# Two more weight places in a pool of their own, so that three output-projection tiles are split ahead of the layer norm's operands

## The chip, the cores and the metric

The kernel runs on one core of one Trainium2 chip. The metric is device time in microseconds (us) from one launch to its end. Three runs of the kernel before gave 1234.79, 1235.42 and 1237.09 us, a median of 1235.42 us. The profile is one further execution, with its own time.

## The reference

The reference is one step of a two-layer encoder over 576 rows: 512 frames of a new stream and 64 frames of a running one. Layer 0 mixes time with a causal depthwise convolution, layer 1 with stick-breaking attention, and each is followed by a SwiGLU feed-forward. The change touches the convolution module, which in the reference is:

```python
def conv_module(xn, prefix, w_in, b_in, w_dw, b_dw, ln_g, ln_b, w_out, b_out):
    a, gate = jnp.split(xn @ w_in + b_in, 2, axis=-1)
    u = a * jax.nn.sigmoid(gate)
    u_ext = jnp.concatenate([prefix.astype(u.dtype), u], axis=1)
    y = lax.conv_general_dilated(u_ext, w_dw[:, None, :], window_strides=(1,), padding='VALID', ...) + b_dw
    y = jax.nn.silu(layernorm(y, ln_g, ln_b))
    return y @ w_out + b_out, u_ext[:, -CONV_STATE:]
```

`D_MODEL` is 1024, the convolution has 31 taps, and all inputs are float32. The output projection `y @ w_out` needs every one of the 1024 layer-normed channels for each of its outputs, and no channel is layer-normed before the sums over all 1024 are known.

## The kernel before

**Layout.** Everything lies transposed: channels on the 128 partitions, the 576 rows of time along the free axis. 1024 channels are 8 chunks `c` (or `m`, for outputs). A product's 576 columns are taken as two halves of 288.

**Split operands.** A float32 product is made of three fp32r products. Each operand x is a rounded high part and the rest, x = xh + xl, and the matmuls are wh·xh, wh·xl and wl·xh. So one weight chunk against one operand chunk is 3 × 2 = 6 matmuls of 128x288 (`mm_ops`, line 591). The weights are split on the chip as they come: a raw tile of 128x1024 lands by DMA in one of the places `wr0` to `wr2` (`load_raw`, line 313). From there it is split in two *units* of 128x512: ScalarE (ACT) writes the high part `wh` (line 509), and VectorE (DVE) subtracts it from the raw weights into `wl` (line 519). With a free PSUM bank a first ACT copy goes to the bank `hp` (line 514), and DVE reads that. A unit sits in a place `w0` to `w3` (tiles `wh0`/`wl0` and so on) until the last matmul that reads it has run.

**Places.** `free["w"]` lists the free places. `advance` takes a place for the next unit as soon as the matmuls of an earlier tile are in the program; `place_for` gives out only places named in `WPOOL` for units *ahead*, those that belong to the next section of the program, because `WPOOL` tiles live in a pool `wpool` that outlasts a section. Section 0 is the projection `w_in`, the convolution and the layer norm. Section 1 is the output projection `w_out` and feed-forward 0, in which `ffn` adds two places, `w4` and `w5`, from its own pool `act0`, which takes over the memory of the convolution's pool. One tile is two units, so 4 places hold two tiles of `w_out`.

**Order.** The instructions are recorded as operations with costs, and `Plan` lays each engine's order out ahead, section by section, from these costs. Engines run their own queues in that order and wait by semaphores. The cost `"next"` (line 1266) stands in the plan of section 0 for the work that TensorE (PE) will find behind each layer-normed chunk.

**Section 0.** For each chunk, `project` makes the gate and value products `pg` and `pa`, `gate` and `glu` make `u`, and the 31 taps are either done on DVE (`acc`, line 1045) and, in part, on ACT and GpSimd (`pr`, `pacc`, lines 1059 and 1062), or on PE (`py`, chunks 4, 5, 7). Then PE sums over channels into `cl` (line 978). ACT and DVE make the mean (`nmp`) and the inverse root (`rp`) of 152 sums from it, and PE spreads both over time (`nm`, `rt`, line 1185). Between these PE runs products of ones, `warm` (line 774), that nobody reads. Then each chunk c is normed: DVE adds the mean (line 1228) and multiplies by the root (line 1236) into `zf`, ACT takes the silu (line 1240) and the high part `zh` (line 1246), and DVE, or GpSimd for chunks 2, 4 and 6, takes the low part `zl` (line 1250). Chunk 0 goes in two halves.

**Section 1.** `w_out_tile` makes the output tiles `po_m` in the order 0, 4, 1, 5, 2, 6, 3, 7, each from all 8 chunks `zh`/`zl`, and adds them to `h` (line 741). The gate and up products `pg` (line 591, then `j_A`, `j_B`, `j_C`, line 1404) follow.

Of the kernel before, what the change touches and what calls it, by code (L numbers as in the profile page):

```python
# [10 lines left out]
P = 128  # L11
# [80 lines left out]

ALONE = (1, 7, 6, 4, 5, 2, 3)
WPOOL = {f"{q}{i}" for q in ("w", "wh", "wl") for i in range(4)} | {f"wr{i}" for i in range(3)}
N_S = 4

FIRST = ((("b0", "b1"), ("b4", "b5")), (("b4", "b5"), ("b0", "b1")))
# [121 lines left out]
def build(tc, xT, vec, st, stp, bdp, wt, ck, cv, w_in, w_out, gu, down, wk, wv, wq, wo, yT, csp, css, kp, ks, vp, vs):  # L219
# [5 lines left out]
    wpool = ctx.enter_context(tc.tile_pool(name="wpool", bufs=1))  # L225
    xpool = ctx.enter_context(tc.tile_pool(name="xpool", bufs=1))
    kpool = ctx.enter_context(tc.tile_pool(name="kpool", bufs=1))
    dram = ctx.enter_context(tc.tile_pool(name="dram", bufs=1, space=bass.MemoryType.DRAM))
    psum = []

# [83 lines left out]

    def wide(tag):

        return wpool if tag in WPOOL else cur[0]

    vecs = base.tile([P, NV], F32, name="vecs")
    nc.sync.dma_start(vecs[:, :V_DW], vec[:, :V_DW])  # L320
# [39 lines left out]
    def dve(n, ptr=False):  # L360
        return n / 960 + (0.13 if ptr else 0.07)
# [4 lines left out]
    def pe(n):  # L366
        return n * 0.000442 + 0.004
# [17 lines left out]


    lo_eng = ["DVE"]
    free = {"wr": [], "w": ["w0", "w1", "w2", "w3"], "S": []}
    pos = {"src": 3, "unit": 0, "tile": 0, "end": 0}
    raw_at = {i: f"wr{i}" for i in range(3)}  # L390
    unit_at, last_use = {}, {}
# [6 lines left out]
    def place_for(q, ahead):  # L398

        for t in free[q]:  # L400
            if not ahead or t in WPOOL:
                free[q].remove(t)
                return t

# [143 lines left out]
    def section():  # L548

        pos["end"] += 1  # L550
        hbanks.clear()
        for q in free:
            free[q] = [t for t in free[q] if t in WPOOL]

    def by_part(tag):
        return [(tag, 0), (tag, 1)]
# [407 lines left out]
        phase_sums(c)  # L964

    stats, psums = [], []

    def stat(parts, dep, i, bias=0.0):

# [15 lines left out]
    def phase_sums(c):  # L985

        k = POLY.index(c)
        et, sqt = f"ye{k % 2}", "zq1" if psums else "zq0"
        es = [et] + [(et, b) for b in range(2)]
        if c == LAST:  # L990
            for b in range(2):

                def f(b=b):
                    if not b:
                        tile(("sq", c), "zq1", (P, Q, QW))
                    nc.scalar.activation(X[("sq", c)][:, 2 * b : 2 * b + 2, :], X[("ye", c)][:, 2 * b : 2 * b + 2, :], AF.Square)

                def pair(key, b=b):
                    x = X[(key, c)]
                    o = tile((key + "2", c, b), f"{key}2{b}", (P, QW))  # L1000
                    nc.vector.tensor_tensor(o, x[:, 2 * b, :], x[:, 2 * b + 1, :], op=ALU.add)

                op("ACT", act(2 * QW, False), f, reads=[(et, b), et] + ["zq1"] * b, writes=[("zq1", b)] + ["zq1"] * (not b), urgent=True)
                for i, (key, deps) in enumerate((("ye", [et, (et, b)]), ("sq", ["zq1", ("zq1", b)]))):
                    op("DVE", dve(QW), lambda key=key, pair=pair: pair(key), reads=deps, writes=[f"{key}2{b}"], urgent=True, port=True)
                    stat([((lambda: sum_of), (lambda key=key, b=b: X[(key + "2", c, b)]))], [f"{key}2{b}"], i)
            return
        op("ACT", act(YW, False), lambda: nc.scalar.activation(tile(("sq", c), sqt, (P, Q, QW)), X[("ye", c)], AF.Square), reads=es, writes=[sqt])
        psums.append(c)
        a = psums[0]  # L1010
        if len(psums) == 2:
            ea = f"ye{POLY.index(a) % 2}"
            op("Pool", pool(YW), lambda: nc.gpsimd.tensor_tensor(tile(("yes",), "yes", (P, Q, QW)), X[("ye", a)], X[("ye", c)], op=ALU.add),
               reads=es + [ea] + [(ea, b) for b in range(2)], writes=["yes"])
        elif len(psums) > 2:
            op("Pool", pool(YW), lambda: nc.gpsimd.tensor_tensor(X[("yes",)], X[("yes",)], X[("ye", c)], op=ALU.add), reads=es, writes=["yes"])
        if len(psums) > 1:
            op("Pool", pool(YW), lambda: nc.gpsimd.tensor_tensor(X[("sq", a)], X[("sq", a)], X[("sq", c)], op=ALU.add), reads=[sqt], writes=["zq0"])
        if len(psums) == len(POLY) - (LAST in POLY):
            for i, (key, tag) in enumerate(((("yes",), "yes"), (("sq", a), "zq0"))):  # L1020
                for n in (2, 1):

                    def f(key=key, n=n):
                        x = X[key]
                        nc.gpsimd.tensor_tensor(x[:, 0:n, :], x[:, 0:n, :], x[:, n : 2 * n, :], op=ALU.add)

                    op("Pool", pool(n * QW), f, writes=[tag])
                stat([((lambda: sum_of), (lambda key=key: X[key][:, 0, :]))], [tag], i)
# [234 lines left out]


    for c in range(NC):
        op("next", 6 * pe(HA) * 2, None, reads=[("z", c, "h"), ("z", c, "l"), ("z", c, "h", 1), ("z", c, "l", 1)], writes=["next"])
    flush()
    section()
    conv_pool.close()
# [169 lines left out]
    def ffn(l, mixer, g_next, nrm_next, x_busy, k_busy):  # L1439
# [1 line left out]
        ap = pool_.enter_context(tc.tile_pool(name=f"act{l}", bufs=1, reuse_waits="tile"))  # L1441
        cur[0] = ap
        free["wr"].append("wr3")
        free["w"] += [f"w{i}" for i in range(4, N_W)]
        free["S"] += [f"S{i}" for i in range(N_S)]
        spots["f"] = [f"f{i}" for i in range(N_F)]
        spots["x"] = [t for t in XT if t not in x_busy]
# [351 lines left out]

    nkv = Norm("kv")  # L1800
    ffn(0, w_out_tile, V_KVG, nkv, XT, [])


    att_pool = ExitStack()
# [641 lines left out]
```

## Time and profile before

| | us |
|---|---|
| runs of the kernel before | 1234.79, 1235.42, 1237.09 (median 1235.42) |
| the profiled execution | 1235.88, of which the span from first to last instruction is 1234.1 |
| PE busy over the span | 1208.9 |
| DVE, ACT, GpSimd busy | 981.4, 979.9, 769.0 |
| granted TensorE clock, mean | 0.994 |

The profile names an engine, a line of the kernel, an operation and tiles (out<-in). In a timeline row the first number is the start and the second how long the row's instructions took, from the first one's start to the last one's end; `x` counts them. A bracket gives the idle time of the engine just before the row and what ended it. Rows of one engine overlap by up to some tenths, since an instruction is recorded to its end while the next has begun; the distance between two starts is what counts in a sum. PE is also pipelined: a product of 288 columns shows 0.42 us for two, while two follow each other at 0.265 us. One MATMUL record of a float32 product of ones stands for a part of it, so that these have more records than instructions.

### The profile page before, as it was taken

To read this page: it belongs to the slowest core of one execution; us is meant where nothing else is said; L and a number is where in the kernel's file an instruction comes from. 1 tells how busy PE (TensorE), PEld (TensorE's weight loads), DVE (VectorE), ACT (ScalarE), POOL (GpSimd) and SP (SyncE) were. 2 spreads that over 40 slices of the span, in tenths; PEclk is the share of its full clock that TensorE was granted. 3 is DMA by queue.
4 is the path that set the end of the run, shared out by engine and by line. 5 is a ranking of instruction groups with operands and counts; after the bars stand their busy time and mean duration, and the time that the engine had idled before them with its cause. 6 is when DMAs were issued, how large, how long until landed. Compare 5 with 4: busy or idle time off the path is not lost.

```text
span 1234.1 us, 24243 instructions
## 1 busy us (share of the span) xinstructions
PE 1208.9 (98%) x8934; PEld 1188.7 (96%) x8934; DVE 981.4 (80%) x1597; ACT 979.9 (79%) x1878; POOL 769.0 (62%) x636
## 2 busy tenths in 40 slices
PE   9999989999999999999999999998999999999996
PEld 8999989999999999999999999998999999999996
DVE  6999976967665669886788999999866566699965
ACT  7998464699887988687668999956988888896873
POOL 1999813469767757865204555554877768677732
PEclk9999989999999999999999999999999999999999
DMA  7333813133232333223373232232232232332222
GB/s 267 88 93 97 261 53 90 52 103 104 69 123 83 96 93 103 87 69 104 111 205 72 48 87 65 53 103 60 78 116 90 79 122 75 99 107 89 84 69 78
DMA packets 46023, 121.10 MB, mean 98 GB/s; under 512 B 8784, under 2 KB 16272, under 8 KB 45904
## 3 DMA queue, kind: packets, MB, share of 16 engines
q1 hardware_dynamic: 45904, 119.56, 32.4%
q8 instruction: 70, 1.15, 0.4%
q14 instruction: 49, 0.40, 0.1%
HBM read 105.18 MB, written 5.70 MB: 90 GB/s over the span
## 4 chain that ended last, share of the span: by engine, by line
PE 80%; DVE 9%; ACT 1%; issue 1%; POOL 0%; DVEq 0%; ACTq 0%
PE j_A L1404 29%; PE j_B L1404 14%; PE j_C L1404 7%; PE pd L591 7%; PE po L591 4%; PE pq L591 4%; PE b L2182 4%; PE pw L591 2%; PE b L2118 2%; DVE acc L1045 2%; PE b L2210 2%; PE pg L591 1%; PE pv L1933 1%; DVE wl L519 1%; PE pk L591 1%; DVE xs L1504 1%
## 5 line engine op out<-in xcount | busy, mean ns | idle before, releaser
L509 ACT ACTIVATE wh<-wr 128x512 fp32r<-128x512 f32 (+1 forms) x303 | 184.2, 613 | 38.0 <-PE po L591 16.1
L519 DVE TENSOR_TENSOR wl<-wr,hp 128x512 fp32r<-128x512 f32 (+1 forms) x241 | 159.0, 664 | 53.4 <-ACT hp L514 52.9
L519 DVE TENSOR_TENSOR wl<-S,hp 128x512 fp32r<-128x512 f32 x226 | 152.7, 682 | 42.8 <-ACT hp L514 40.1
L509 ACT ACTIVATE wh<-S 128x512 fp32r<-128x512 f32 x228 | 141.1, 627 | 29.0 <-PE pd L591 10.4
L514 ACT ACTIVATE hp<-wr 128x512 fp32r<-128x512 f32 (+1 forms) x241 | 139.1, 579 | 23.7 <-DVE wl L519 19.9
L514 ACT ACTIVATE hp<-S 128x512 fp32r<-128x512 f32 x226 | 133.9, 596 | 13.0 <-POOL S L439 8.1
L439 POOL TENSOR_TENSOR S<-wr,wr 128x512 f32<-128x512 f32 x57 | 76.8, 1348 | 92.5 <-DMA wr<-gu 24.7
L1062 POOL TENSOR_TENSOR pacc<-pacc,pr 128x608 f32<-128x608 f32 x69 | 109.0, 1594 | 7.3 <-ACT pr L1059 4.1
L475 POOL TENSOR_TENSOR S<-wr,S 128x512 f32<-128x512 f32 x57 | 78.5, 1378 | 32.9 <-DVE wl L519 19.0
L439 POOL TENSOR_TENSOR S<-wr 128x512 f32<-128x512 f32 x57 | 78.7, 1382 | 26.3 <-DVE wl L519 10.4
L439 POOL TENSOR_TENSOR S<-S,wr 128x512 f32<-128x512 f32 x57 | 77.9, 1369 | 12.2 <-DVE wl L519 5.7
L1581 POOL TENSOR_TENSOR a<-a,r 128x576 f32<-128x576 f32 x44 | 67.0, 1525 | 15.1 <-DVE a L1558 15.1
L1581 POOL TENSOR_TENSOR t<-t,r 128x576 f32<-128x576 f32 x44 | 66.5, 1513 | 9.5 <-ACT t L1552 8.2
L591 PE MATMUL pd<-ap,wh 128*128 128x288 f32 x384 | 66.0, 294 | 0.0
L1045 DVE SCALAR_TENSOR_TENSOR acc<-u,vecs,acc 128x608 f32<-128x608 f32 x76 | 64.8, 853 | 1.0
L1059 ACT ACTIVATE pr<-u,vecs 128x608 f32<-128x608 f32 x69 | 54.2, 798 | 8.1 <-POOL pacc L1062 7.8
L1587 DVE TENSOR_TENSOR a<-a,t 128x576 f32<-128x576 f32 x44 | 49.2, 1119 | 11.2 <-ACT t L1585 10.9
L591 PEld LDWEIGHTS pd<-ap,wh 128*128 128x128 f32 x384 | 56.0, 188 | 0.0
L519 DVE TENSOR_TENSOR wl<-wr,wh 128x512 fp32r<-128x512 f32 x62 | 49.8, 814 | 6.8 <-ACT wh L509 6.7
L1552 ACT ACTIVATE t<-j_A 128x288 f32<-128x288 f32 x84 | 34.1, 407 | 22.7 <-PE j_A L1404 21.8
L1673 DVE TENSOR_TENSOR h<-j_A,h 128x288 f32<-128x288 f32 x60 | 27.2, 455 | 18.9 <-PE j_A L1404 18.6
L2084 POOL TENSOR_TENSOR e<-t,e 128x512 fp32r<-128x512 f32 (+1 forms) x20 | 27.1, 1355 | 22.7 <-DVE e L2080 12.0
(854 smaller groups left out, 4511.7 us busy)
## 6 DMA issues: line engine op xcount, KB each, us to landing
wr<-gu SPq DMA_DIRECT2D x88, 512.0 KB, 3.6
wr<-down SPq DMA_DIRECT2D x32, 512.0 KB, 3.8
wr<-w_in SPq DMA_DIRECT2D x15, 512.0 KB, 3.8
wm<-wt SPq DMA_DIRECT2D x12, 576.0 KB, 6.3
wr<-down SPq DMA_DIRECT2D x16, 384.0 KB, 3.2
qd<-qd SPq DMA_DIRECT2D x21, 256.0 KB, 3.2
wr<-w_out SPq DMA_DIRECT2D x8, 512.0 KB, 3.6
wr<-wq SPq DMA_DIRECT2D x8, 512.0 KB, 4.0
```

Of the source, the lines that this page charges most:

```text
L439: eng(e).tensor_tensor(t[:, :n], x[1](), y[1](), op=ALU.subtract if sub else ALU.add)
L475: eng(e).tensor_tensor(v[:, :n], X[("raw", i0)][:, n : 2 * n], v[:, :n], op=ALU.subtract)
L509: nc.scalar.activation(X[("w", u)][0][:, :n], get(), AF.Copy)
L514: nc.scalar.activation(t[:, :n], get(), AF.Copy)
L519: eng(le).tensor_tensor(b[:, :n], get(), a.bitcast(F32)[:, :n], op=ALU.subtract)
L591: nc.tensor.matmul(o[hf], (hi, hi, lo)[j][:, s], (xh, xl, xh)[j], start=(start and q == 0 and j == 0), stop=(stop and q == n - 1 and j == 2),)
L1045: nc.vector.scalar_tensor_tensor(dst, src, wt_, dst if i else X[("kneg",)], op0=ALU.mult, op1=ALU.add)
L1059: nc.scalar.activation(tile(("pr", c, i), f"pr{m}", (P, YW)), src, AF.Copy, scale=wt)
L1062: nc.gpsimd.tensor_tensor(X[("pacc", c)], X[("pacc", c)], X[("pr", c, i)], op=ALU.add)
L1404: nc.tensor.matmul(out, a[:, s], b, start=(start and q == 0 and i == 0), stop=(q == len(ops_) - 1 and i == 2), skip_group_check=True,)
L1581: nc.gpsimd.tensor_tensor(X[k], X[k], r, op=ALU.mult)
L2182: nc.tensor.matmul(zz()[:, a : a + n], X[("trir",) if same else ("oner",)], X[key][:, x, c : c + n], start=False, stop=(i == len(mms) - 1) ...
```

## The change

Two places, `w4` and `w5`, move from the pool of section 1 into a pool of their own, `wpool2`, that is open from the start until the end of section 1. Places of it are given out from the start of section 0, and to units ahead while section 0 is laid out. In section 3 the second feed-forward adds `w4` and `w5` from its own pool, as before. To make room, four small tiles of the last chunk's sums (`ye20`, `sq20`, `ye21`, `sq21`) are laid in the places of four other small tiles that the layer norm writes later (`vs`, `rs`, `rp`, `nmp`). The cost `"next"` goes from 6 to 9 matmul pairs. No arithmetic is changed, and as many units are split as before.

```diff
 WPOOL = {f"{q}{i}" for q in ("w", "wh", "wl") for i in range(4)} | {f"wr{i}" for i in range(3)}
+
+WPOOL2 = {f"{q}{i}" for q in ("w", "wh", "wl") for i in (4, 5)}
...
+    w_pool2 = ExitStack()
+    wpool2 = w_pool2.enter_context(tc.tile_pool(name="wpool2", bufs=1))
...
-        return wpool if tag in WPOOL else cur[0]
+        return wpool if tag in WPOOL else wpool2 if tag in WPOOL2 and pos["end"] < 2 else cur[0]
...
-    free = {"wr": [], "w": ["w0", "w1", "w2", "w3"], "S": []}
+    free = {"wr": [], "w": [f"w{i}" for i in range(N_W)], "S": []}
...
-            if not ahead or t in WPOOL:
+            if not ahead or t in WPOOL or (t in WPOOL2 and not pos["end"]):
...
-            free[q] = [t for t in free[q] if t in WPOOL]
+            free[q] = [t for t in free[q] if t in WPOOL or (t in WPOOL2 and pos["end"] < 2)]
...
+    SMALL = {("ye", 0): "vs", ("sq", 0): "rs", ("ye", 1): "rp", ("sq", 1): "nmp"}
...
-                    o = tile((key + "2", c, b), f"{key}2{b}", (P, QW))
+                    o = tile((key + "2", c, b), SMALL[key, b], (P, QW))
...
-        op("next", 6 * pe(HA) * 2, None, reads=[("z", c, "h"), ("z", c, "l"), ("z", c, "h", 1), ("z", c, "l", 1)], writes=["next"])
+        op("next", 9 * pe(HA) * 2, None, reads=[("z", c, "h"), ("z", c, "l"), ("z", c, "h", 1), ("z", c, "l", 1)], writes=["next"])
...
-        free["w"] += [f"w{i}" for i in range(4, N_W)]
+        if l:
+            free["w"] += [f"w{i}" for i in range(4, N_W)]
...
     ffn(0, w_out_tile, V_KVG, nkv, XT, [])
+    w_pool2.close()
```

The order of the instructions shows what this moves. The first place is PE's queue where the output projection begins. In a name, `po_4_0` is output tile 4, half 0; `zh1` is the high part of chunk 1; `wh234` is place `wh2` with unit 34 (units 32 and 33 are the tile for output 0, 34 and 35 that for output 4, 36 and 37 that for output 1). Each row stands for the six matmuls that open with it. Before:

```order
L591 MATMUL po_0_0_2068<-zh0_1981,wh032_1535 128x288
...
L591 MATMUL po_4_0_2070<-zh0_1981,wh234_1572 128x288
...
L591 MATMUL po_0_0_2068<-zh1_2003,wh032_1535 128x288
...
L591 MATMUL po_0_0_2068<-zh2_2006,wh032_1535 128x288
...
L591 MATMUL po_0_0_2068<-zh3_2017,wh032_1535 128x288
...
L591 MATMUL po_4_0_2070<-zh1_2003,wh234_1572 128x288
```

The same place with the change:

```order
L595 MATMUL po_0_0_2081<-zh0_1994,wh232_1396 128x288
...
L595 MATMUL po_4_0_2083<-zh0_1994,wh434_1540 128x288
...
L595 MATMUL po_1_0_2085<-zh0_1994,wh036_1586 128x288
...
L595 MATMUL po_0_0_2081<-zh1_2007,wh232_1396 128x288
...
L595 MATMUL po_4_0_2083<-zh1_2007,wh434_1540 128x288
...
L595 MATMUL po_1_0_2085<-zh1_2007,wh036_1586 128x288
```

Behind chunk 0 there were 12 matmuls and now there are 18, those of output 1 among them; the same holds for chunk 1. Before, all of output 1 stood behind the last matmul of outputs 0 and 4. Now its chunks 2 and 3 stand among those of outputs 0 and 4, and its chunks 4 to 7 behind them.

The second place is DVE's queue in the same stretch, where the low part of chunk 1, `zl1`, is made. Before:

```order
L1236 TENSOR_TENSOR zf_2_1986<-rt_1_1963,zf_2_1986 128x288
L1228 TENSOR_TENSOR zf_3_1996<-y_3_1712,nm_1901 128x512
L1228 TENSOR_TENSOR zf_3_1996<-y_3_1712,nm_1901 128x64
L1228 TENSOR_TENSOR zf_4_2000<-y_4_1835,nm_1901 128x512
L1228 TENSOR_TENSOR zf_4_2000<-y_4_1835,nm_1901 128x64
L1236 TENSOR_TENSOR zf_3_1996<-rt_0_1962,zf_3_1996 128x288
L1236 TENSOR_TENSOR zf_3_1996<-rt_1_1963,zf_3_1996 128x288
L1236 TENSOR_TENSOR zf_4_2000<-rt_0_1962,zf_4_2000 128x288
L1236 TENSOR_TENSOR zf_4_2000<-rt_1_1963,zf_4_2000 128x288
L1250 TENSOR_TENSOR zl1_2004<-zf_1_1976,zh1_2003 128x576
```

With the change:

```order
L1233 TENSOR_TENSOR zf_2_2004<-y_2_1469,nm_1914 128x64
L1233 TENSOR_TENSOR zf_3_2010<-y_3_1754,nm_1914 128x512
L1233 TENSOR_TENSOR zf_3_2010<-y_3_1754,nm_1914 128x64
L1241 TENSOR_TENSOR zf_2_2004<-rt_0_1975,zf_2_2004 128x288
L1241 TENSOR_TENSOR zf_2_2004<-rt_1_1976,zf_2_2004 128x288
L1255 TENSOR_TENSOR zl1_2008<-zf_1_1989,zh1_2007 128x576
```

`zl1` now stands ahead of the addition for chunk 4 and the multiplications for chunks 3 and 4, and ACT's queue likewise takes `zh1` straight behind the silu of chunk 1.

The third place is DVE's queue at the start of section 0, between the root `r` of the first norm and the first taps of chunk 0's convolution (`acc_0`). `wl04` is place `wl0` with unit 4. Before:

```order
L519 TENSOR_TENSOR wl04_306<-wr2_89,hp_4_307 128x512
L519 TENSOR_TENSOR wl26_335<-wr3_245,hp_6_336 128x512
L836 TENSOR_TENSOR sg_0_362<-pg_0_143,r_97 128x576
L519 TENSOR_TENSOR wl15_359<-wr2_89,hp_5_360 128x512
L870 TENSOR_TENSOR pa_0_145<-pa_0_145,r_97 128x576
L880 SCALAR_TENSOR_TENSOR u_0_134<-pa_0_145,vecs_73,sg_0_362 128x512
L880 SCALAR_TENSOR_TENSOR u_0_134<-pa_0_145,vecs_73,sg_0_362 128x64
L519 TENSOR_TENSOR wl37_391<-wr3_245,hp_7_392 128x512
L1047 TENSOR_SCALAR acc_0_423<-u_0_134,vecs_73 128x608
```

With the change:

```order
L523 TENSOR_TENSOR wl44_294<-wr2_92,wh44_293 128x512
L523 TENSOR_TENSOR wl06_318<-wr3_248,hp_6_319 128x512
L523 TENSOR_TENSOR wl55_327<-wr2_92,wh55_326 128x512
L523 TENSOR_TENSOR wl28_352<-wr4_273,hp_8_353 128x512
L840 TENSOR_TENSOR sg_0_375<-pg_0_146,r_100 128x576
L523 TENSOR_TENSOR wl17_372<-wr3_248,hp_7_373 128x512
L874 TENSOR_TENSOR pa_0_148<-pa_0_148,r_100 128x576
L884 SCALAR_TENSOR_TENSOR u_0_137<-pa_0_148,vecs_76,sg_0_375 128x512
L884 SCALAR_TENSOR_TENSOR u_0_137<-pa_0_148,vecs_76,sg_0_375 128x64
L523 TENSOR_TENSOR wl39_404<-wr4_273,hp_9_405 128x512
L1052 TENSOR_SCALAR acc_0_436<-u_0_137,vecs_76 128x608
```

Units 8 and 9, the third tile ahead, are split ahead of the first taps; from here to the end of section 0, every unit is split one tile earlier in the sequence than before. Behind the last sums `cl` in PE's queue stand 4 `warm` products now, where 8 stood; the other four stand ahead of these sums.

4 lines of the change are left out of this document (2 added, 2 removed).

## The prediction

> **What bounds the kernel now.** I read the page first, then busy times by stage, then the rows of the stage that the change touches.
>
> ```profile
> PE 1208.9 (98%) x8934; PEld 1188.7 (96%) x8934; DVE 981.4 (80%) x1597; ACT 979.9 (79%) x1878; POOL 769.0 (62%) x636
> ...
> 93.00:124.00 31.00, 30.71 (x232) 30.51 (x231) 30.61 (x43) 27.79 (x42) 30.45 (x22) 1.00 0.35 102
> 124.00:155.00 31.00, 29.15 (x220) 28.25 (x219) 29.81 (x44) 12.34 (x17) 25.05 (x20) 1.00 0.84 259
> 155.00:186.00 31.00, 27.53 (x181) 26.01 (x180) 24.73 (x55) 21.01 (x34) 4.73 (x3) 0.83 0.19 54
> ```
>
> Columns of a stage: its stretch and length, then busy us of PE, PE's weight loads, DVE, ACT, GpSimd, then the granted clock. PE is busy 98% of the span, so a saving must come from PE's idle or slow time. The stretch 155 to 186 us has most of both: 3.5 us idle and a mean clock of 0.83. Ahead of it, the convolution is DVE's: 30.61 of 31 us. So work taken off PE's waits at 162 us is worth its full length, and DVE work added ahead of 155 us costs its full length.
>
> The stage in detail, PE alone by the microsecond (busy, clock):
>
> ```profile
> 163.00:164.00 1.00, 0.93 (x4) 0.69 0.83 328
> 166.00:167.00 1.00, 0.32 (x2) 0.50 0.00 0
> 168.00:169.00 1.00, 0.00 (x0) 0.50 0.00 0
> 173.00:174.00 1.00, 1.00 (x7) 0.69 0.00 0
> ```
>
> 0.69 in a microsecond is a change between 1.00 and 0.50 at 0.38 of it: the clock was halved from 163.38 to 173.38, 10.0 us. PE's rows:
>
> ```profile
> 162.23 0.40 PE L591 MATMUL po<-zh,wh 128*128 128x288 f32 x1 [0.80 <-ACT zh L1246]
> ...
> 165.42 0.68 PE L591 MATMUL po<-zh,wl 128*128 128x288 f32 x2
> 166.79 0.85 PE L591 MATMUL po<-zh,wh 128*128 128x288 f32 x2 [0.68 <-ACT zh L1246]
> 169.47 0.85 PE L591 MATMUL po<-zl,wh 128*128 128x288 f32 x2 [1.83 <-DVE zl L1250]
> 170.11 0.68 PE L591 MATMUL po<-zh,wl 128*128 128x288 f32 x2
> 170.59 0.68 PE L591 MATMUL po<-zh,wh 128*128 128x288 f32 x2
> ...
> 174.07 0.42 PE L591 MATMUL po<-zh,wl 128*128 128x288 f32 x2
> 174.33 0.43 PE L591 MATMUL po<-zh,wh 128*128 128x288 f32 x2
> ```
>
> Two matmuls follow each other at 0.48 us at half clock (170.11 to 170.59) and at 0.265 us at full clock (174.07 to 174.33): 0.24 and 0.1325 us each. After the 12 matmuls of chunk 0 PE runs dry at 165.9, gets two matmuls at 166.79, and waits for `zl1` until 169.47. From there it never waits in this stage. The third tile, output 1, is done when DVE adds it to `h`:
>
> ```profile
> 188.80 0.94 DVE L741 SCALAR_TENSOR_TENSOR h<-po,vecs,h 128x288 f32<-128x288 f32 x2 [1.93 <-PE po L591]
> ```
>
> Three tiles are 3 × 8 × 6 = 144 matmuls, 19.1 us at full clock. From 162.23 that would end at 181.3; it ended at 188.75. So 7.4 us are lost here, 30 slow matmuls (30 × 0.1075 = 3.2 us) and about 4.1 us of waiting. That is the most this stage can give.
>
> **The change: what it saves.** Behind chunk 0 stand 18 matmuls, not 12. The added six run from 165.9 at 0.24 us, to 167.3. Is chunk 1 there by then? DVE's rows, and ACT's silu and high part of one chunk:
>
> ```profile
> 162.21 0.46 DVE L1250 TENSOR_TENSOR zl<-zf,zh 128x288 fp32r<-128x288 f32 x1
> 162.58 0.81 DVE L1228 TENSOR_TENSOR zf<-y,nm 128x512 f32<-128x512 f32 x2
> 163.31 0.45 DVE L1250 TENSOR_TENSOR zl<-zf,zh 128x288 fp32r<-128x288 f32 x1
> 163.68 1.55 DVE L1236 TENSOR_TENSOR zf<-rt,zf 128x288 f32<-128x288 f32 x4
> 165.14 1.92 DVE L1228 TENSOR_TENSOR zf<-y,nm 128x512 f32<-128x512 f32 x4
> ...
> 168.43 0.98 DVE L1250 TENSOR_TENSOR zl<-zf,zh 128x576 fp32r<-128x576 f32 x1
> ...
> 177.74 0.76 DVE L1250 TENSOR_TENSOR zl<-zf,zh 128x576 fp32r<-128x576 f32 x1 [1.75 <-ACT zh L1246]
> ...
> 172.02 0.87 ACT L1240 ACTIVATE zf<-zf,vecs 128x576 f32<-128x576 f32 x1 [1.42 <-DVE zf L1236]
> 172.92 0.69 ACT L1246 ACTIVATE zh<-zf 128x576 fp32r<-128x576 f32 x1
> ```
>
> Between starts, an addition of chunk 2 is 0.73 us (162.58 to 163.31), a chunk's multiplication 0.73 (four halves from 163.68 to 165.14), a half `zl` 0.38. In the new order DVE does, from 162.58: the multiplication of chunk 1 (to 163.31), the second half `zl0` (163.7), the additions of chunks 2 and 3 (165.2), the multiplication of chunk 2 (165.9), then `zl1` (0.7 to 0.8, to 166.7). ACT has `zh1` at 163.31 + 0.90 + 0.69 = 164.9. So chunk 1 is whole at 166.7, not 169.4, and PE, at 167.3, does not wait for it. The two waits (0.9 and 2.2 us in the rhythm of the matmuls) go.
>
> The clock. From 169.47 PE had work without a break, and the clock was back at 173.38: 3.9 us. With the change PE has unbroken work from about 163.3 on, so I take 167.2 for its return; the bound on the other side is the 10.0 us of before, 173.4.
>
> Late next is DVE. It does the same work in the stage, so `zl7` is whole as before, at 177.74 + 0.76 = 178.5. The new queue holds behind it the last four matmuls of output 0 and six groups of six (output 4's chunks 6 and 7, output 1's chunks 4 to 7): 40 × 0.1325 = 5.3 us, to 183.8. PE's own sum agrees: 162.23 + 19.1, plus 16 slow matmuls up to 167.2 (1.7 us), plus the 0.8 us of gaps in chunk 0's halves, is 183.8. With some tenths for chunks 3 and 5, which land just as PE asks, output 1 ends at 184.1, not 188.75: **4.6 us**. Bounds: 7.4 us if no wait and no slow matmul were left, and with the clock slow to 173.4 (42 slow matmuls, 4.5 us) 186.6, so 2.1 us.
>
> [...]
>
> **What it costs.** As many units are split as before, but two more of them before the convolution, where DVE is the bound:
>
> ```profile
> 24.49 0.69 DVE L519 TENSOR_TENSOR wl<-wr,hp 128x512 fp32r<-128x512 f32 x1 [2.21 <-ACT hp L514]
> 25.09 0.75 DVE L836 TENSOR_TENSOR sg<-pg,r 128x576 f32<-128x576 f32 x1
> ...
> 28.68 0.85 DVE L1047 TENSOR_SCALAR acc<-u,vecs 128x608 f32<-128x608 f32 x1
> ...
> 23.85 0.60 ACT L514 ACTIVATE hp<-wr 128x512 fp32r<-128x512 f32 x1 [2.82 <-DMA wr<-w_in]
> 24.39 0.62 ACT L509 ACTIVATE wh<-wr 128x512 fp32r<-128x512 f32 x1
> ...
> DVE wl L519 <- ACT hp L514: 3.0, 3, 2.2
> ```
>
> A subtraction takes 0.60 us of DVE (24.49 to 25.09), so two take 1.2 us ahead of the first tap at 28.68. All four subtractions ahead of the gate now stand in a row there. The fourth needs ACT's fourth instruction after 23.85, at some 0.53 us each, so at 26.05, while DVE is free at 25.7: 0.3 us more. The last row (waits of DVE in the first 156 us: in total, times, longest) shows 0.8 us in two later waits, which earlier splitting may hide. So the convolution ends 0.7 to 1.5 us later; I take **1.3 us**, near the upper end, since no row shows these two waits going. GpSimd (30.45 of 31) starts and ends later by as much. What leaves the later stage, two ACT and two DVE instructions at 177.6 us, stood beside a busy PE: nothing.
>
> At nothing I also cost: each `w_out` tile's DMA one tile earlier (the DMA engines are at 0.35 in 93 to 124); the four shared small tiles (their new writers wait for `cl` on PE, which reads the old contents, as before); `w4` and `w5` outside `act0`.
>
> The warm products: 8 behind the last sums keep PE busy up to the mean's spreading.
>
> ```profile
> 155.94 1.95 PE L774 MATMUL warm<-ones 128*128 128x128 f32 x16
> 157.72 1.92 PE L1185 MATMUL nm<-nmp,row_of 128*128 128x72 f32 x16
> 159.48 1.95 PE L1185 MATMUL rt<-rp,row_of 128*128 128x72 f32 x16
> ```
>
> With 4, PE idles some 0.85 us (half of 157.72 − 155.94) ahead of `nm`. Itself free, since `nm` waits for ACT. If it makes the clock fall ahead of `rt`, `rt` takes up to 1.8 us longer, and chunk 0 comes that much later. Between 0 and 1.8 I take 0: an equal idle time, 0.80 us at 162.23, was followed by the fall, but so close to it that I cannot say which idle time counts.
>
> Sum: −4.6 + 1.3 = **−3.3 us**. The profiled execution took 1235.88 us, 0.46 above the median, so 1232.6 for it and **1232.1** for the median.
>
> Does the lead last to the end? Behind the stage PE is full:
>
> ```profile
> 300.00:400.00 100.00, 100.00 (x757) 1.00 0.31 96
> ...
> POOL S L439 <- DMA wr<-gu: 29.7, 14, 5.0
> ```
>
> PE is full there, and GpSimd, which starts each weight sum, waits 29.7 us for raw tiles, whose places come free as PE goes on. What feeds PE follows PE.
>
> **The rivals.** *The clock stays slow longer, or falls earlier.* With the 10.0 us of before the saving is 2.1 − 1.3 = 0.8 us, 1234.6; with `rt` slowed by 1.8 us, 4.6 − 1.3 − 1.8 = 1.5 us, 1233.9. For it: the stretch 163.4 to 166.1, nearly full, did not restore the clock before, and the idle time ahead of `nm` is new. Against: PE is now without a break far longer. Chance 0.22. [...]
>
> *The lead is spent downstream.* ACT or GpSimd limits the first feed-forward, and PE waits there for what it gained: 1.3 us slower to 3.3 us faster, most simply 1236.7 with the whole 4.6 spent and about 1234.4 with half. Against it, the rows just shown. Chance 0.12.
>
> *The subtractions wait in the convolution* (slower). DVE works strictly in its queue's order, and each `wl` waits for its `hp` on ACT. Over the whole kernel such waits are:
>
> ```profile
> DVE wl L519 <- ACT hp L514: 93.0, 130, 2.2
> ```
>
> That is 0.7 us each; section 0 has three. If the new order sets five or more further `wl` ahead of their `hp`, 5 × 0.7 = 3.5 us eat the 3.3; ten make it 7.0 − 3.3 = 3.7 us slower, 1239.1. Against: the order was laid out with the same costs as before, by which 32 such pairs gave three waits. Chance 0.08.
>
> *More than forecast*: the clock never falls and the two waits of 0.8 us are hidden, 1230.5. Chance 0.06. That the third tile is not taken as it comes is ruled out by the order shown above.
>
> **How the numbers follow.** The forecast has 0.52, from 1231.0 to 1233.0. A measurement of this kernel can tell about 0.2%, 2.5 us, from no change, so "faster" means below 1232.95. Nearly all of the forecast and the last rival lie there: 0.55. The clock, the spent lead and a rest of the forecast are within 0.2%: 0.37. The waiting subtractions: 0.08. The range leaves out the last rival's end, the waiting subtractions and the spent lead beyond no gain: 1230.6 to 1235.5.
>
> **What would show it.** In the new profile: no wait of PE behind chunk 0, output 1's addition to `h` 4.6 us sooner after the first `po` matmul (26.6 us before, 22 now); first tap at 30.1 us, first `po` at 163.5; the gate product `pg` starting at 218.4, not 221.70; from there on PE as full as before. Wrong would be a first `po` later than 165 us, a clock below 1.00 for more than 5 us, or a new PE wait behind 220 us.

## The result, and the profile after

The changed kernel is slower, not faster: a median of 1243.53 us over six runs (1241.63 to 1244.71), against 1236.08 us over six runs of the kernel before (1234.79 to 1237.09). The ratio is 1.0059, with a 95% interval of 1.0049 to 1.0069. The forecast was 1232.1 us. The profiled execution took 1243.84 us, with a span of 1242.1 us, 8.0 us more than before.

The lines of the page and of the busy times by stage that answer to those of the prediction (same columns; line numbers of the changed kernel are 4 to 6 higher):

```profile
PE 1207.0 (97%) x8934; PEld 1187.3 (96%) x8934; DVE 984.6 (79%) x1597; ACT 979.8 (79%) x1878; POOL 772.3 (62%) x636
...
93.00:124.00 31.00, 31.00 (x234) 30.82 (x233) 30.15 (x41) 27.70 (x44) 30.29 (x22) 1.00 0.34 92
124.00:155.00 31.00, 27.95 (x211) 27.10 (x209) 28.85 (x45) 12.76 (x18) 26.72 (x22) 1.00 0.83 257
155.00:186.00 31.00, 20.64 (x135) 19.15 (x136) 22.11 (x50) 16.83 (x27) 4.29 (x3) 0.78 0.12 30
```

PE does the same work in all, but in the stretch 155 to 186 us it is busy 20.64 us instead of 27.53, and the mean clock fell from 0.83 to 0.78. PE's timeline there (start, length, instructions; in brackets the idle time before, and what ended it):

```profile
166.70 0.40 PE L595 MATMUL po<-zh,wh 128*128 128x288 f32 x1 [0.79 <-ACT zh L1251]
...
169.19 0.66 PE L595 MATMUL po<-zh,wl 128*128 128x288 f32 x2
178.17 0.82 PE L595 MATMUL po<-zh,wh 128*128 128x288 f32 x2 [8.32 <-DVE zf L1233]
```

After the first 12 matmuls, those of outputs 0 and 4 on chunk 0, PE stands still for 8.32 us. Line 1233 is DVE's addition of the mean. In DVE's timeline the last two of these additions, then the addition of output 1 to `h`, and from the instructions on `pg` the first gate product, with the change and then before (its start is the first of the two times):

```profile
176.11 1.92 DVE L1233 TENSOR_TENSOR zf<-y,nm 128x512 f32<-128x512 f32 x4
...
198.08 0.94 DVE L745 SCALAR_TENSOR_TENSOR h<-po,vecs,h 128x288 f32<-128x288 f32 x2
```

```profile
L595 PE MATMUL pg<-('x', 0, 0)_0_b,wh x16: 292/294/302, 230.9 to 237.8; 128*128 128x288 f32 x16
```

```profile
L591 PE MATMUL pg<-('x', 0, 0)_0_b,wh x16: 292/295/298, 221.7 to 228.6; 128*128 128x288 f32 x16
```

PE goes on when the last addition of the mean is done, at 178.03. The loss is read off three points:

| | before | after | later by |
|---|---|---|---|
| first `po` matmul | 162.23 | 166.70 | 4.5 |
| output 1 added to `h` | 188.80 | 198.08 | 9.3 |
| first gate product `pg` | 221.7 | 230.9 | 9.2 |

So the convolution ends 4.5 us later, and the stage from the first `po` to output 1 takes 31.4 us instead of 26.6, 4.8 us more. Behind it nothing more is lost: at the end 8.0 us are left. Where the other 1.2 us came back stays open.

**Why PE waits there.** In the order with its semaphores, the first matmul of output 1 reads, before and with the change:

```
L591 MATMUL po_1_0_2072<-zh0_1981,wh436_2148 128x288 [waits PE_49,Activation_49]
L595 MATMUL po_1_0_2085<-zh0_1994,wh036_1586 128x288 [waits DVE_49,PE_49]
```

A wait for DVE is new. What can it be? The layer norm's PSUM pool, `pp0`, holds `acc`, `p1` and `p0` (1024 columns each) and `p4`, `p5` (512 each). The mean `nm` lies in `p0`, the root `rt` in `p5` and `p4`. The next pool, `pp1`, takes over the same memory. If its places are handed out in the order of their first use, output 0 gets that of `acc`, output 4 that of `p1` and output 1 that of `p0`. Then output 1's accumulator lies where the mean lies until DVE's last addition has read it. Before, output 1 began behind all of outputs 0 and 4, when the mean was long done. With the change everything behind output 1's first matmul waits too: chunk 1 was whole at 171.09 us (`zl1`, 170.34 + 0.75), but its matmuls for outputs 0 and 4, which stand behind that one in PE's queue, did not start before 178.17. That PE waits for the bank was the theory for the experiments; the rival was that PE waits for weights or for chunks, and that the profile names the wrong releaser.

### The profile page after: what moved, and what is told of

Its sections match the earlier page's. It is cut to its first block, busy times and chain, and to the rows that moved or that the text cites. A ratio compares the mean times of both kernels' runs of the same rounds, so it can differ in the third digit from the quotient of the medians.

```text
span 1242.1 us, 24245 instructions
## 1 busy us (share of the span) xinstructions
PE 1207.0 (97%) x8934; PEld 1187.3 (96%) x8934; DVE 984.6 (79%) x1597; ACT 979.8 (79%) x1878; POOL 772.3 (62%) x636
## 4 chain that ended last, share of the span: by engine, by line
PE 80%; DVE 9%; ACT 4%; POOL 4%; issue 1%; DVEq 0%; POOLq 0%
PE j_A L1409 28%; PE j_B L1409 14%; PE j_C L1409 7%; PE pd L595 7%; PE po L595 4%; PE pq L595 4%; PE b L2189 4%; POOL pacc L1067 3%; PE pw L595 2%; PE b L2125 2%; PE b L2217 2%; ACT pr L1064 2%; DVE acc L1050 2%; PE pg L595 1%; PE pv L1940 1%
## 5 line engine op out<-in xcount | busy, mean ns | idle before, releaser
L479 POOL TENSOR_TENSOR S<-wr,S 128x512 f32<-128x512 f32 x57 | 83.2, 1460 | 42.2 <-ACT wh L513 23.1
L1564 DVE TENSOR_TENSOR t<-j_C,t 128x288 f32<-128x288 f32 x42 | 19.1, 455 | 30.9 <-PE j_C L1409 30.8
```

The source lines that it names most:

```text
L479: eng(e).tensor_tensor(v[:, :n], X[("raw", i0)][:, n : 2 * n], v[:, :n], op=ALU.subtract)
```

## The experiments

**One tile fewer.** Six places stay, but two tiles meet the chunks again:

```diff
-            if not ahead or t in WPOOL or (t in WPOOL2 and not pos["end"]):
+            if not ahead or t in WPOOL:
...
-        op("next", 9 * pe(HA) * 2, ...)
+        op("next", 6 * pe(HA) * 2, ...)
```

> The six weight places stay, from the start of section 0 on, but only w0 to w3 are given to units ahead, and the cost "next" is 6 again: two w_out tiles meet the layer-normed chunks, as before the change. Theory (bank): in the changed kernel the third tile's accumulator lies in the PSUM banks of the spread mean, and PE's 8.32 us wait behind chunk 0 is for the last addition of the mean. Then the wait is gone here; from the first po matmul to output 1's addition to h it is 26 to 27.5 us (before 26.6, with the change 31.4); the first tap stays at 30.4 us and the first po at 166 to 167 us; so 4.8 of the 8.0 us go, about 1239 us (1238 to 1240.5). Rival (weights or chunks): PE waits there for the low parts or the weights, which come as late as in the changed kernel; then a wait of over 5 us remains behind chunk 0, and the time is 1242 to 1245.

Measured: 1240.16 us, ratio 1.0039 (1.0025 to 1.0053). PE's and DVE's timelines:

```profile
165.17 0.40 PE L595 MATMUL po<-zh,wh 128*128 128x288 f32 x1
...
169.73 0.53 PE L595 MATMUL po<-zh,wh 128*128 128x288 f32 x2 [1.65 <-ACT zh L1251]
172.41 0.85 PE L595 MATMUL po<-zl,wh 128*128 128x288 f32 x2 [2.15 <-DVE zl L1255]
```

```profile
192.10 0.94 DVE L745 SCALAR_TENSOR_TENSOR h<-po,vecs,h 128x288 f32<-128x288 f32 x2 [1.98 <-PE po L595]
```

The 8.32 us are gone, the two small waits of before are back, and the stage takes 26.9 us. The convolution still ends late: its first tap came at 29.34 us instead of the 30.4 expected, its first `po` at 165.17, 0.8 us ahead of the expected bound.

**Late places.** The third tile stays, but `w4` and `w5` are withheld from section 0's own projection:

```diff
-            if not ahead or t in WPOOL or (t in WPOOL2 and not pos["end"]):
+            if t in WPOOL or ahead == (t in WPOOL2 and not pos["end"]):
```

> w4 and w5 are given only to units ahead while section 0 is laid out, so that its own projection goes with four places, as before, and the third w_out tile still meets the chunks. Theory (convolution): the 4.5 us by which the convolution ends later come from the two subtractions ahead of the first tap (1.7 us at the tap) and from some 3 us of DVE's waits for ACT in the order that follows; here the first tap is at 28.7 us again, and the first po at 163.3 to 165 us, since two more subtractions (1.2 us) and some waits still stand in the convolution. The bank theory keeps the wait of about 8.3 us behind chunk 0 and 31 to 32 us from the first po to output 1's addition. Time 1241 to 1242.5. Rival: what delays the convolution is the number of units split in it (38, not 36), wherever they stand; then the first po is at 166 to 167 us again, and the time 1243 to 1244.5.

Measured: 1241.24 us, ratio 1.0050 (1.0035 to 1.0065). DVE's first tap and PE's two rows:

```profile
28.01 0.85 DVE L1052 TENSOR_SCALAR acc<-u,vecs 128x608 f32<-128x608 f32 x1
```

```profile
162.61 0.40 PE L595 MATMUL po<-zh,wh 128*128 128x288 f32 x1 [0.79 <-ACT zh L1251]
174.09 0.82 PE L595 MATMUL po<-zh,wh 128*128 128x288 f32 x2 [7.60 <-DVE zf L1233]
```

The wait stays, and the stage takes 30.7 us (output 1 is added at 193.32). The first `po` now comes only 0.4 us later than before, less than either theory said, although 38 units are split in the convolution as in the changed kernel. Part of that is an earlier start of this execution: its first tap comes at 28.01 us instead of 28.68. From the tap to the first `po` it takes 134.60 us, against 133.55 before and 136.33 with the change, so 1.05 us are still lost behind the tap, about what two more subtractions take (1.2 us). So the two losses are separate.

**Other banks.** The places of `pp1` are laid out beforehand, so that output 1 lies on the root instead of the mean:

```diff
     pp = psum_pool("pp1")
+    for tag in ("b4", "b5", "b2", "b3", "b6", "b7", "b0", "b1"):
+        pp.tile([P, 512], F32, name=f"at_{tag}", tag=tag)
```

> The changed kernel with the banks of the second PSUM pool laid out beforehand, so that output 1's accumulator lies in the two banks of the spread root instead of those of the spread mean. Theory (bank): PE stops behind the same 12 matmuls, but until the last multiplication by the root, which in the changed kernel ends at 180.1 us, 2.0 us behind the last addition of the mean; the profile names DVE's multiplication as what ends the wait, which is some 10.3 us long; about 1.5 to 2 us slower than the changed kernel, 1244.5 to 1246. Rival (weights, low parts or high parts of the chunks): nothing of these moves, the wait stays 8.3 us and the time 1242 to 1244.5.

Measured: 1246.51 us (one run), half a microsecond above the expected range. DVE's first tap and PE's timeline:

```profile
29.66 0.85 DVE L1052 TENSOR_SCALAR acc<-u,vecs 128x608 f32<-128x608 f32 x1
```

```profile
165.97 0.40 PE L595 MATMUL po<-zh,wh 128*128 128x288 f32 x1 [0.79 <-ACT zh L1251]
...
179.56 0.82 PE L595 MATMUL po<-zh,wh 128*128 128x288 f32 x2 [10.18 <-DVE zf L1241]
```

No weight and no operand moved, yet the wait grew to 10.18 us and ends with DVE's multiplication by the root (L1241). The bank theory had said 10.3; the rival, 8.3. The place of the accumulator sets this wait. (The first `po` comes 0.7 us earlier than in the changed kernel because the first tap does, 29.66 against 30.37; between the two the kernels agree to 0.02 us.)

**The mean copied out of PSUM.** ACT copies it once, and DVE adds the copy for chunks 1 to 7:

```diff
+    def keep_mean():
+        nc.scalar.activation(tile(("nms",), "u3", (P, T)), X[("nm",)][:, O0 : O0 + T], AF.Copy)
+
+    op("ACT", act(T), keep_mean, reads=NT, writes=["u3"], urgent=True)
...
-                m = X[("nm",)][:, O0 + a : O0 + b]
+                m = X[("nms",)][:, a:b] if c >= 1 else X[("nm",)][:, O0 + a : O0 + b]
```

> The changed kernel, with the mean copied once from PSUM to SBUF by ACT, ahead of its first silu; chunks 1 to 7 add the copy, so that the banks are free some 1 us behind the mean's spreading. Theory (bank): no wait over 2 us behind chunk 0; 22 to 24 us from the first po to output 1's addition (the 22.0 of the forecast, against 31.4 now); the convolution still ends 4.5 us later than before; so the two nearly cancel, 1234.5 to 1237 us, within 0.2% of the kernel before. Rival (weights or chunks): the wait stays above 5 us and the time above 1241. Second rival: the clock stays slow in this stage whatever the wait, then 24 to 26 us and 1237 to 1239.

Measured: 1235.67 us, ratio 1.000 (0.9991 to 1.001). ACT's and DVE's timelines, and PE's first row:

```profile
163.29 0.65 ACT L1219 ACTIVATE nms<-nm 128x576 f32<-128x576 f32 x1 [0.50 <-PE nm L1190]
...
163.97 0.82 DVE L1238 TENSOR_TENSOR zf<-y,nm 128x512 f32<-128x512 f32 x2 [1.37 <-ACT nms L1219]
...
166.41 0.40 PE L595 MATMUL po<-zh,wh 128*128 128x288 f32 x1 [1.37 <-ACT zh L1256]
```

```profile
171.47 3.65 DVE L1238 TENSOR_TENSOR zf<-y,nms 128x512 f32<-128x512 f32 x4
...
177.15 3.26 DVE L1238 TENSOR_TENSOR zf<-y,nms 128x512 f32<-128x512 f32 x4
...
189.65 0.94 DVE L745 SCALAR_TENSOR_TENSOR h<-po,vecs,h 128x288 f32<-128x288 f32 x2
```

PE no longer stops, and output 1 follows the first `po` by 23.2 us: 8.1 us less than in the changed kernel. The late convolution takes it all back. Two prices of the copy show. DVE's first addition waits for ACT's copy, though both only read (1.37 us of idle time, 0.69 without the copy, on the path to chunk 0), and two groups of four later additions, those of chunks 4 and 5 and of chunks 6 and 7, take 3.65 and 3.26 us, where the changed kernel, which reads the mean from PSUM, has 2.31 and 1.92.

**Both cures together**, the edit of the late places and that of the copied mean:

> Both cures together: w4 and w5 go only to units ahead while section 0 is laid out (e2_places_late), and the mean is copied to SBUF ahead of ACT's first silu (e4_mean_copy). Theory: the two costs were independent, so they go together: first po at about 163.2 us (162.6 of e2_places_late and 0.6 for chunk 0's addition, which waits for the copy), output 1's addition to h 23.2 us later, as in e4_mean_copy, at 186.4 us, 2.4 us ahead of before (188.80); 1233 to 1234.5 us. Rival (the lead is spent downstream): 1235 to 1236 although output 1 is added at 186.4.

Measured: 1234.06 us, ratio 0.998 (0.997 to 0.9989); first `po` at 163.54, output 1 at 186.76. The two losses add up, so the two cures do.

**The copy behind chunk 0**, so that chunks 0 and 1 add the mean from PSUM:

```diff
+        if c == 2:
+            op("ACT", act(T), keep_mean, reads=NT + [("zk", 0, 1)], writes=["u3"], urgent=True)
```

> As e5_copy_late, but ACT copies the mean behind both halves of chunk 0, and chunks 2 to 7 add the copy; chunks 0 and 1 add the mean from PSUM. Theory: chunk 0 no longer waits for the copy, so the first po is at 162.6 us; output 1's addition 22.5 to 23.5 us later (DVE's additions of two SBUF operands still stretch beside GpSimd's low parts), at 185 to 186; 1232 to 1233.7 us, the forecast's size. Rival: the copy ahead of chunk 1's silu delays chunk 1, the wait returns in part, and output 1 is added no earlier than 186.4.

Measured: 1233.53 us, ratio 0.9977 (0.9967 to 0.9986). The first `po` came at 163.02 and output 1 was added at 186.59, 23.6 us later. GpSimd's and PE's timelines:

```profile
174.34 2.70 POOL L1258 TENSOR_TENSOR zl<-zf,zh 128x576 fp32r<-128x576 f32 x1 [3.71 <-ACT zh L1254]
```

```profile
177.09 0.53 PE L595 MATMUL po<-zl,wh 128*128 128x288 f32 x2 [1.09 <-POOL zl L1258]
```

Half a microsecond went to the earlier start as expected, but PE now waits 1.09 us for GpSimd's low part of a chunk, so the stage gained nothing over the copy ahead of chunk 0. The time is the one that the theory expected, but output 1 came as late as the rival had said (no earlier than 186.4), and a wait did return, though not at chunk 1.

**The low parts on DVE** (`ZL_POOL = ()` in place of `(2, 4, 6)`, the rest as in the last kernel):

> As e6_copy_later, with the low parts of chunks 2, 4 and 6 made on DVE, so that GpSimd does nothing in this stage. It tells whether GpSimd's low parts stretch DVE's additions of two SBUF operands: in e4_mean_copy four additions took 3.65 and 3.26 us, in the changed kernel, with the mean in PSUM, 2.31 and 1.92. Theory (port): each four take 2 x 0.75 us again or little more, 1.5 to 2.0 us; DVE gains some 2.6 us by it and does 3 x 0.73 us more, so the time is within 0.5 us of e6_copy_later. Rival (the copy's place in SBUF is slow by itself): the additions stay at 3.2 us or more, and the time is 1 to 2 us above e6_copy_later.

Measured: 1232.96 us, ratio 0.9974 (0.9963 to 0.9984), the lowest median of all, though its interval overlaps that of the last kernel. PE's and DVE's timelines:

```profile
162.56 0.40 PE L595 MATMUL po<-zh,wh 128*128 128x288 f32 x1 [0.79 <-ACT zh L1254]
```

```profile
167.79 1.30 DVE L1236 TENSOR_TENSOR zf<-y,nms 128x512 f32<-128x512 f32 x2
...
173.66 2.01 DVE L1236 TENSOR_TENSOR zf<-y,nms 128x512 f32<-128x512 f32 x4
...
184.91 0.94 DVE L745 SCALAR_TENSOR_TENSOR h<-po,vecs,h 128x288 f32<-128x288 f32 x2
```

The additions of chunks 6 and 7 take 2.01 us beside an idle GpSimd, and took 3.26 beside one of its subtractions, from the same place in SBUF. Those of chunks 4 and 5, a pair each here, take 1.30 and 1.27 us, where the four together took 3.65. The stage takes 22.35 us, and PE's timeline marks no wait in it behind the first row.

**Six places from unit 12 on**, to find what delays the convolution. Only the two early subtractions are put off:

```diff
-            if not ahead or t in WPOOL or (t in WPOOL2 and not pos["end"]):
+            if t in WPOOL or (t in WPOOL2 and not pos["end"] and pos["unit"] >= 12) or (not ahead and not (t in WPOOL2 and not pos["end"])):
```

> The changed kernel with w4 and w5 withheld until unit 12, so that only the two subtractions ahead of the first tap are put off; from then on section 0 has six places. Theory: the convolution's 4.5 us are the 1.7 us at the first tap and some 3 us of DVE's waits for ACT in the order behind it; here the tap is at 28.0 to 28.8 us; if the waits belong to six places, the first po is at 164.5 to 165.5 us, and if they belong to the order that the early subtractions brought, at 162.5 to 163.5. PE's wait behind chunk 0 stays at about 8 us; 1241 to 1243 us. Rival (nothing but the number of splits counts): first po at 166 to 167 us.

Measured: 1245.93 us (one run), above the expected range. The first tap came at 28.20, earlier than before, and still the first `po` at 166.67. A part of that is the slow clock (0.50 from 163.52 us on), which came during the spreading of the root in PE's timeline (1.95 us in the changed kernel):

```profile
163.29 3.41 PE L1190 MATMUL rt<-rp,row_of 128*128 128x72 f32 x16
```

Ahead of it, DVE reads the last sums (the first instruction on `vs`) at 160.27, against 160.94 in the changed kernel and 156.47 before, so the convolution itself ends 3.8 us later than before. The theory of the two subtractions falls: without them ahead of the tap the convolution is nearly as late. The first `po` met the rival's forecast, but the number of splits alone is not the cause either, as the experiment with late places had shown.

**The plan told of the bank**: no copy, but output 1 is planned behind the mean's last addition (on top of the late places):

```diff
         tag = (("b4", "b5"), ("b2", "b3"), ("b0", "b1"))[i % 3]
...
+        if i == 2:
+            op("PE", 0.0, lambda: None, writes=both("p0") + list(tag))
```

> As e2_places_late (mean in PSUM, no copy), but the plan is told that output 1's accumulator lies where the mean lies: its first matmul is planned behind the last addition of the mean, and the chunks 1 to 3 of outputs 0 and 4 go ahead of it. Theory (bank): the banks are the limit and not PE's order alone; PE no longer stands still for 8 us with other work queued, but the third tile also no longer fills the gap behind chunk 0; so the stage is about as before the change: waits of 1 to 3 us behind chunk 0 again, 26 to 28 us from the first po to output 1's addition (26.6 before, 31 in e2_places_late), 1236 to 1237.8 us with the first po at 162.6 to 163.2. Rival (the early third tile is worth its 4 us even behind the last addition): 23 to 25 us and 1233 to 1235.

Measured: 1238.80 us, ratio 1.0020 (1.0011 to 1.003). First `po` at 162.76, output 1 added at 189.50, 26.7 us later. The stage is as before the change (26.6 us), as the bank theory says: a third tile that had to wait for its place was worth nothing. The time missed the expected range by 1 us. Its profiled execution, at 1236.32 us the shortest of ten, lies inside; what the others lost is not seen in it.

**Another order for the same work.** The plan's cost of each DVE instruction is raised by 0.02 or 0.03 us, once with late places and once in the changed kernel:

```diff
-        return n / 960 + (0.13 if ptr else 0.07)
+        return n / 960 + (0.16 if ptr else 0.09)
```

> What is still open is why the convolution ends later with six places. e2_places_late with the plan's cost of every DVE instruction raised by 0.02 to 0.03 us: no instruction is added or removed, w4 and w5 go only to units ahead, but all engines get another order in the convolution. Theory (six places cost): section 0 with four places ends its convolution early in any order laid out from these costs, so the first po is at 162 to 164 us. Rival (each order has its own losses, and before's was a lucky one): the first po moves by 2 us or more, to 165 us or later. The bank wait behind chunk 0 stays, 7 to 9 us; by the theory 1240 to 1242.5 us, by the rival 1243 or more.

> The changed kernel with the same shift of the plan's DVE costs: six places from the start, another order in the convolution. Theory (six places cost): first po at 165 to 168 us, 2 us or more later than in e10_late_dve; 1242 to 1245.5 us. Rival (each order has its own losses): no such distance to e10_late_dve, with the first po anywhere from 162.5 to 168 us; if it comes at 164 us or earlier, six places cost nothing by themselves.

Measured: 1257.12 and 1258.53 us (one run each). PE's first `po`, with late places and then with six from the start:

```profile
172.40 0.40 PE L595 MATMUL po<-zh,wh 128*128 128x288 f32 x1 [0.79 <-ACT zh L1251]
```

```profile
172.28 0.61 PE L595 MATMUL po<-zh,wh 128*128 128x288 f32 x1
```

Both moved, by 9.8 and 5.6 us, and the 4 us between four and six places vanished. So six places don't cost 4 us in any order: each order has its own losses, as the rival said, and the one of before is better than both of these. The rival's range was missed, though (172.28 us in the second kernel, where it had said 168 at most), and in the second kernel the clock was already slow (0.50 from 167.57 us on) when the root was spread (3.62 us instead of 1.95), so its 5.6 us are not the order's alone; its last sum of the convolution on DVE (`ys`) starts 2.6 us later than in the changed kernel, 9.5 us later in the first than with late places. Both new orders come from higher costs (0.62 us for a 128x512 subtraction, which the traces show at 0.60, as the old cost has it). Whether such costs lead to worse orders in general was not tested. In the first of the two, DVE's waits in the convolution and its busy time in two stretches (30.50 and 30.61 before) show the loss:

```profile
DVE wl L523 <- ACT hp L518: 6.6, 6, 1.9
DVE u L884 <- ACT sg L844: 2.2, 2, 1.1
DVE acc L1050 <- ACT kneg L1130: 1.7, 1, 1.7
```

```profile
62.00:93.00 31.00, 29.88 (x220) 28.82 (x219) 25.72 (x36) 26.47 (x42) 30.45 (x22) 1.00 0.34 101
93.00:124.00 31.00, 30.33 (x226) 29.70 (x225) 26.53 (x38) 28.45 (x44) 29.90 (x21) 1.00 0.33 92
```

The whole times of these two can't be compared with the others, since the new costs lay out the later sections anew too.

## Why the prediction was wrong

**The step that failed** is the one that begins "Behind chunk 0 stand 18 matmuls, not 12. The added six run from 165.9". It asked when the chunks and the clock would be there, and who is late next, and answered "DVE". It never asked where the six matmuls write. Their accumulator lay on the mean, DVE's last reader of it comes at the end of the stage, and the added six held up all that PE had queued behind them. In place of −4.6 us the term was +4.8 us. None of the rivals held this case. Two of the prediction's own signs of being wrong came: a first `po` later than 165 us, and a clock that was slow for more than 5 us (13.65). The sentence that would have led to it stood in the kernel (`"p0"` for the mean, a new pool that opens behind it), and the semaphores of the row showed the wait.

**The mechanism without the bank was right, and so was its size in this stage.** With the mean out of the way, late places and GpSimd idle beside DVE's additions, the stage took 22.35 us from the first `po` to output 1, where the forecast had 22.0, and the kernel 1232.96 us, where it had 1232.1. That the whole times agree so well is luck in part: that kernel also has three further edits, its stage gave 4.2 us and not 4.6, its convolution cost 0.3 us and not 1.3, and the kernel before, run beside it, had a median of 1236.39 us and not 1235.42. That the lead lasts was right too: output 1 was 3.9 us ahead of before in that kernel, and the median 3.4 us.

**The convolution's term was mis-sized:** 4.5 us, not 1.3. The main part of the forecast was the subtractions ahead of the first tap, and these came nearly as expected (the tap at 30.37, forecast 30.1). DVE's first subtraction from `hp` and the first tap in the changed kernel:

```profile
24.61 0.69 DVE L523 TENSOR_TENSOR wl<-wr,hp 128x512 fp32r<-128x512 f32 x1 [2.07 <-ACT hp L518]
...
30.37 0.85 DVE L1052 TENSOR_SCALAR acc<-u,vecs 128x608 f32<-128x608 f32 x1
```

From the one to the other it takes 5.76 us, against 4.19 before: 1.57 us, where the forecast had 1.5. But ACT's `hp`, for which the first of them waits, comes at another time in each execution. In the four profiled kernels with this same order ahead of the tap (the changed kernel, one tile fewer, other banks, the copied mean) the tap came at 30.37, 29.34, 29.66 and 29.53 us, always 5.75 or 5.76 us behind that row. So a first `po` read from one execution is uncertain by about 1 us; the 2.8 us behind the tap are not, as two executions agree on them (136.33 and 136.31 us from the tap to the first `po` in the changed kernel and with other banks, 133.55 before).

The other part, DVE's waits later in the convolution, was taken to shrink, since "earlier splitting may hide" them. Instead they grew. DVE's waits between 28 and 157 us, in the changed kernel and then before:

```profile
DVE wl L523 <- ACT hp L518: 1.9, 4, 1.1
DVE u L884 <- ACT sg L844: 1.2, 2, 1.0
DVE sq L1080 <- ACT sq L1086: 0.4, 1, 0.4
DVE pa L874 <- PE pa L595: 0.3, 1, 0.3
```

```profile
DVE vs L1192 <- ACT vs L1191: 2.0, 1, 2.0
DVE wl L519 <- ACT hp L514: 0.8, 2, 0.6
```

Without `vs`, which stands behind the last tap, that is 3.8 us instead of 0.8, and accounts for the 2.8 us beyond the tap's 1.7. The rival of the waiting subtractions had the right kind of cost, but put it on `wl` alone, which explains 1.1 of the 3.0. As the perturbed orders showed, such a term can't be worked out by counting instructions: the added work was 1.2 us, while two orders of the same work differed by 9.8. Which pairs of instructions cost the 4.5 us in the changed order stays open.

**What held.** `zl1` was whole 4.4 us after the first `po` (170.34 + 0.75, against 166.70; forecast 4.5):

```profile
170.34 0.75 DVE L1255 TENSOR_TENSOR zl<-zf,zh 128x576 fp32r<-128x576 f32 x1
...
163.96 1.95 PE L1190 MATMUL rt<-rp,row_of 128*128 128x72 f32 x16
```

The fewer warm products behind the last sums cost nothing: `rt` takes 1.95 us, as before. PE is as full as before behind the stage. The clock's return was forecast 5.0 us after the first `po`; where PE wasn't blocked it came after 4.7 (167.28 against 162.56). One row was misread: 0.69 in the microsecond from 173 puts the clock's return at 0.62 of it, 173.62, so that it was slow for 10.2 us and not 10.0, and back 4.2 us after 169.47 and not 3.9. By the rows about 28 matmuls ran slow in that time, not 30. Neither changes the forecast by more than some tenths.

## What to carry to other kernels

Work that is moved earlier needs the place of its output earlier too: for each instruction that a change moves ahead, ask who last reads the memory that it writes, above all where one pool takes over from another and a planner's keys don't connect the two. In the changed kernel one such wait, of 8.32 us, held up all that PE had queued behind it, so work that couldn't start was worse there than work that stood later: the stage took 31.4 us instead of 26.6. And where a list scheduler lays out the order of a full stage, a change of 1.2 us of work cost 4.5 us here, of which 2.8 came through the order behind it, and new plan costs for the same work cost 9.8. So hold the order still, as far as possible, where only another part is to be changed: with the late places, 1 us was lost behind the tap.

## What was not expected of the hardware

The slow clock came in whole steps. Read off the granted clock (0.50 where it is slow) of half-microsecond stretches from 150 to 190 us, it was slow in the profiled executions for 3.41 us (four kernels with the copy, the fourth 3.42), 6.83 (plan told of the bank), 10.24 (before, and 10.23 with one tile fewer), 13.65 (changed kernel, and late places), 17.07 (other banks) and 20.48 us (six places from unit 12 on): one to six times 3.41. In the two kernels with raised costs it was slow for 13.66 us from 174.30 us on, with late places, where an earlier slow stretch was over at 150.41, and for 23.90 with six: four and seven times. Where two falls of one execution are seen, they lie whole steps apart (at 153.50 and 170.57 us with one tile fewer: five steps; at 160.74 and 167.57 us with raised costs and six places: two). In the changed kernel, with stretches of that length laid from the fall on (PE busy, then the clock):

```profile
169.20:172.61 3.41, 0.65 (x4) 0.50 0.00 0
172.61:176.03 3.42, 0.00 (x0) 0.50 0.00 0
176.03:179.44 3.41, 1.27 (x5) 0.50 0.00 0
179.44:182.85 3.41, 3.41 (x16) 0.50 0.00 0
```

Here the clock returns at the end of the first stretch in which PE is busy throughout. Such a stretch was not always enough: with six places from unit 12 on PE was busy from the fall at 163.52 to the end of the first stretch at 166.93, and with raised costs and six places from the fall at 167.57 to 170.98, and the clock came back only at 184.00 and 188.05. Nor did a stretch have to be full: with late places the clock came back after one with 3.11 us busy, while 3.09 us did not bring it back with six places from unit 12 on. The busy time does not tell the fall either: in the stretch that ended with it, PE was busy 2.35 of 3.41 us in the changed kernel, while one in the convolution with 2.21 busy kept the clock. What sets the fall and the return stays open.

```profile
152.13:155.55 3.42, 2.21 (x18) 1.00 0.47 105
...
165.79:169.20 3.41, 2.35 (x13) 1.00 0.55 154
```

Two further points came out of the copy. DVE's additions of two SBUF operands stretched beside GpSimd's subtractions, as shown above: four additions lost 1.25 us (3.26 against 2.01), beside a subtraction of GpSimd that takes 1.44 us in the changed kernel, and GpSimd's own subtraction took up to 2.70 us beside them. Which instruction waited for which is not seen in the runs. And DVE's first addition waited for ACT's copy (1.37 us of idle time, 0.69 without the copy), although neither writes the mean. The trace shows the wait, and not its cause. So this copy belonged behind the reader that is on the path: behind chunk 0 it gave back 0.5 us (first `po` at 163.02 us, against 163.54).
